# A third plain feature tile in each feed-forward, wide sums of its second half, and modulation weights in larger transfers

## The chip, the cores and the metric

The kernel runs on one core of a Trainium2 chip. The metric is the device time of one launch in microseconds (us), as the median of several runs. Besides, one execution was recorded by the hardware profiler; all rows below come from it. The engines are TensorE (PE: matmuls, with PEld for its weight loads), VectorE (DVE: elementwise operations), ScalarE (ACT: activations, copies, casts), GpSimd (POOL) and SyncE (SP: it issues the transfers, in order).

## What is computed

One step of a diffusion backbone of two layers, on 512 latent and 128 context tokens of width 1024, all in fp32. Each layer is a feed-forward (FFN), a mixer of three groups of heads, and a second FFN. Norm, shift, scale and gate of every part are modulated by vectors that come from a conditioning vector and a large matrix `w_ada`:

```python
def swiglu(x, w_in, w_out):
    g, u = jnp.split(x @ w_in, 2, axis=-1)
    return (jax.nn.silu(g) * u) @ w_out

def layer(h, mod, p, lam_init, ctx):
    sh1, sc1, gt1, sh2, sc2, gt2, sh3, sc3, gt3 = jnp.split(mod[:, None, :], 9, axis=-1)
    u = rmsnorm(h, p["g_norm"][0]) * (1.0 + sc1) + sh1
    h = h + 0.5 * gt1 * swiglu(u, p["w_ff_in"][0], p["w_ff_out"][0])
    ...
    y, cache = mix(u, p, lam_init, ctx)
    h = h + gt2 * y
    ...
    h = h + 0.5 * gt3 * swiglu(u, p["w_ff_in"][1], p["w_ff_out"][1])

for l in range(DEPTH):
    mod_ctx = jax.nn.silu(c_ctx)[None, :] @ w_ada[l] + b_ada[l]
    mod_lat = jax.nn.silu(c) @ w_ada[l] + b_ada[l]
```

Here x is 640 x 1024, w_in 1024 x 5632, w_out 2816 x 1024, and w_ada 1024 x 9216 per layer.

## The kernel before, in words

The four FFNs are called FFN0 to FFN3 here, in the order in which they run; FFN0 lies between the start and 537 us, FFN1 between 958 and 1436, FFN2 between 1436 and 1916, FFN3 between 2338 and 2806, and the two mixers between them.

Every matmul is done as three, on a high and a low part of both operands (`mm3`, L187): H x H, H x L, L x H. High parts are casts on ACT, low parts subtractions on DVE. So each operand, weight or activation, passes through ACT and DVE before PE can use it.

The first product of an FFN goes by 22 feature tiles f of 128 features (gate and up), in `GROUPS` of 6, 6, 5 and 5; after each group comes the second product of that group, in four steps of two output tiles (`unit2`). The 640 tokens are two halves of 320 (half 0, half 1), and the 1024 rows of the weights two halves of four k each. Two ways are used for a feature tile:

- *plain*, for tiles 0 and 1 of each FFN: eight quarter products, 96 matmuls of 320 columns. `plain0` does half 0 (from B11 and B21, 24 matmuls each, kk = 0 and 1), and `plain1` half 1 (from T1 and B22, 48 matmuls). `plain_copy` parks the result of B11 in the tiles `pm`, since half 1 needs it again; `plain_add` adds it. The weights are split in two pieces of 1024 columns (`split`).
- *wino*, for all others: seven products instead of eight, 84 matmuls, in exchange for sums of weights on DVE: seven splits of 512 columns (`split4`) and four sums of 512 columns (`weights`, L949).

What both need of the activations are sums too: `u_steps` (L761) makes them, for half 1 the tiles T1, B22, T3, T2, T4, each as a high and a low part, per k in pieces of 128 x 320. Plain tiles need T1 and B22 only, wino tiles all.

Before the first feature tile of FFN1, 2 and 3 the norm of half 1 isn't done yet. It is a generator, `self.pend`: its first step puts the sum of squares on PE (nst), its second puts the row of factors on PE (nbc) and then emits all `u_steps` (nx is the first operation on DVE). `ffn` takes the two steps between the chunks of `plain0`. After a plain product th is the tanh (ACT) and the gating (DVE, L685 and L686), hid the split of the result.

Modulation: 72 units of 256 columns of w_ada a layer are needed, 8 of them in the startup, others in two ways. A unit by P is eight *strips* on PE (`ada_strip`, adp<-adaw, one for each k, narrow weights of 32 columns), a copy by ACT (adrow) and two small matmuls that fold it (adt). A unit by D is 16 multiply-adds on DVE (adacc, L342 and L344), then transposes on PE (adt). Their weights come through `ada_raw` (L320) in the tiles adaw; the page counts 256 transfers of 256 KB. The table `ADA` gives, by FFN, at which feature tile (first entry) and at which step of the second product (second entry) `pump` emits units, and of which sort.

The order on each engine is set by a scheduler at build time (and in the startup by a planner of its own, with costs and due times); each engine runs its list in order. PE has two slots for the tiles gu, and the weights four slots each of H and L. SP issues transfers in order and waits where the buffer is still in use.

## Time and profile before

| | us |
|---|---|
| median of 3 runs (2825.23 to 2825.39) | 2825.35 |
| the profiled execution | 2820.54 |
| span of its trace | 2818.8 |
| PE busy | 2707.1 |
| DVE busy | 2158.1 |
| ACT busy | 1298.7 |
| POOL busy | 310.8 |

The span goes from the first to the last instruction; the profiled execution's own time is a little more. [...] In the timelines neighbouring instructions of a kind are one row with a count; a number in square brackets is the time that the engine stood idle before it, followed by what released it.

### The profile page before, as it was taken

How to read it: one execution, taken by the hardware profiler on the slowest of the kernel's cores; microseconds unless marked ns; L12 is line 12 of the kernel's file. 1: busy time of each engine (PE TensorE's matmuls, PEld its weight loads, DVE VectorE, ACT ScalarE, POOL GpSimd, SP SyncE). 2: the span in 40 equal slices, each digit the busy share in tenths (PEclk: the TensorE clock that was granted, in tenths of full speed). 3: DMA queues.
4: the chain of work that ended last, by engine and by line, in shares of the span. 5: the costliest groups of instructions: out<-in, count | busy, mean ns of one | idle time of the engine just before them, and what ended most of it. 6: DMA issues, size and time to landing. Idle time of an engine off the chain costs nothing.

```text
span 2818.8 us, 47166 instructions
## 1 busy us (share of the span) xinstructions
PE 2707.1 (96%) x17821; PEld 2526.0 (90%) x17821; DVE 2158.1 (77%) x4717; ACT 1298.7 (46%) x3001; POOL 310.8 (11%) x505
## 2 busy tenths in 40 slices
PE   6999999999989999999989999999999998999998
PEld 5799999888889889999979999997888897999998
DVE  6688889766865598899979989888667647776765
ACT  5324334456666352433444334345657634443433
POOL 1000000142522100000010000003343220000000
PEclk8999999999999999999999999999999999999999
DMA  8443443322102334343343433442211032322232
GB/s 241 143 143 113 128 124 112 113 92 87 39 3 81 93 94 131 91 120 117 109 120 105 120 117 99 133 129 83 82 49 38 3 109 79 90 75 75 83 83 76
DMA packets 365403, 276.47 MB, mean 98 GB/s; under 512 B 27176, under 2 KB 352888, under 8 KB 365176
## 3 DMA queue, kind: packets, MB, share of 16 engines
q1 hardware_dynamic: 365176, 273.46, 32.8%
q8 instruction: 141, 2.31, 0.4%
q14 instruction: 86, 0.70, 0.1%
HBM read 259.25 MB, written 14.16 MB: 97 GB/s over the span
## 4 chain that ended last, share of the span: by engine, by line
PE 80%; DVE 9%; DMA 4%; ACT 3%; issue 2%; POOL 2%; SPq 0%; DVEq 0%; POOLq 0%; ACTq 0%
PE gu L191 33%; PE w L191 17%; PE zps L191 6%; PE ga L191 5%; PE wo L191 4%; PE tr L1276 3%; PE y L191 3%; DMA adaw<-in_w_ada 3%; PE sc L191 2%; PE num L191 2%; DVE adacc L344 1%; PE adp L332 1%; PE z L191 1%; DVE h L928 1%; DMA out_new_b_n<-cst 1%
## 5 line engine op out<-in xcount | busy, mean ns | idle before, releaser
L191 PE MATMUL w<-hid,wH 128*128 128x384 f32 (+1 forms) x2816 | 625.2, 312 | 0.8 <-ACT hid L691 0.4
L191 PE MATMUL gu<-u,wH 128*128 128x320 f32 x3392 | 594.0, 316 | 28.2 <-DVE th L686 21.3
L191 PEld LDWEIGHTS gu<-u,wH 128*128 128x128 f32 x3392 | 519.8, 190 | 60.8 <-DVE th L686 22.5
L191 PE MATMUL gu<-u,wL 128*128 128x320 f32 x3136 | 548.5, 314 | 6.2 <-ACT X L1003 3.3
L191 PEld LDWEIGHTS gu<-u,wL 128*128 128x128 f32 x3136 | 479.9, 189 | 28.9 <-ACT X L1003 10.6
L191 PEld LDWEIGHTS w<-hid,wH 128*128 128x128 f32 x2816 | 472.5, 188 | 5.6 <-ACT hid L691 3.9
L191 PE MATMUL w<-hid,wL 128*128 128x256 f32 (+1 forms) x1408 | 433.5, 310 | 0.0
L344 DVE SCALAR_TENSOR_TENSOR adacc<-adaw,cs,adacc 128x256 f32<-128x256 f32 x602 | 269.5, 480 | 14.6 <-DMA adaw<-in_w_ada 11.0
L220 ACT CAST wH<-raw 128x512 fp32r<-128x512 f32 x280 | 172.4, 620 | 219.0 <-PE w L191 87.4
L191 PEld LDWEIGHTS w<-hid,wL 128*128 128x128 f32 x1408 | 265.0, 189 | 0.3
L220 ACT CAST wL<-raw 128x512 fp32r<-128x512 f32 x280 | 172.8, 620 | 167.7 <-PE gu L191 43.0
L736 POOL TENSOR_TENSOR ssum<-ssum,sq 128x384 f32<-128x384 f32 (+1 forms) x36 | 36.2, 1004 | 1914.4 <-ACT sq L735 1861.0
L191 PE MATMUL zps<-wH,u 128*128 128x512 f32 x704 | 244.2, 407 | 1.8 <-ACT u L885 1.7
L928 DVE SCALAR_TENSOR_TENSOR h<-w,mod,h 128x128 f32<-128x128 f32 (+1 forms) x384 | 154.9, 435 | 101.6 <-PE w L191 100.2
L221 DVE TENSOR_TENSOR wH<-raw,wH 128x512 fp32r<-128x512 f32 x280 | 191.8, 686 | 34.5 <-ACT wH L220 33.8
L221 DVE TENSOR_TENSOR wL<-raw,wL 128x512 fp32r<-128x512 f32 x280 | 191.9, 687 | 32.1 <-ACT wL L220 29.1
L211 ACT CAST wH<-raw 128x768 fp32r<-128x768 f32 (+2 forms) x140 | 112.2, 802 | 200.9 <-PE w L191 168.0
L191 PEld LDWEIGHTS zps<-wH,u 128*128 128x128 f32 x704 | 133.3, 190 | 33.8 <-ACT u L885 5.3
L691 ACT CAST hid<-th 128x320 fp32r<-128x320 f32 x176 | 80.9, 459 | 165.3 <-DVE th L686 165.3
L212 DVE TENSOR_TENSOR wL<-raw,wH 128x768 fp32r<-128x768 f32 (+2 forms) x140 | 127.7, 916 | 21.7 <-PE gu L191 15.9
L191 PE MATMUL zps<-wL,u 128*128 128x512 f32 x352 | 139.2, 395 | 0.0
L1684 DVE TENSOR_REDUCE mx<-sc 128x1 f32<-128x640 f32 (+1 forms) x160 | 110.7, 708 | 27.2 <-PE sc L191 26.8
(338 smaller groups left out, 4492.4 us busy)
## 6 DMA issues: line engine op xcount, KB each, us to landing
raw<-in_w_ff_in SPq DMA_DIRECT2D x176, 512.0 KB
adaw<-in_w_ada SPq DMA_DIRECT2D x256, 256.0 KB
raw<-in_w_ff_out SPq DMA_DIRECT2D x32, 768.0 KB
raw<-in_w_ff_out SPq DMA_DIRECT2D x32, 640.0 KB
rawi<-in_w_in SPq DMA_DIRECT2D x16, 1024.0 KB
adaw<-in_w_ada SPq DMA_DIRECT2D x16, 512.0 KB
rawo<-in_w_out SPq DMA_DIRECT2D x8, 1024.0 KB
bspill<-z SPq DMA_DIRECT2D x20, 256.0 KB
```

The lines of the kernel that those rows point to most:

```text
L191: self.nc.tensor.matmul(out, lhsT, rhs, start=start, stop=stop, skip_group_check=go_on)
L211: nc.scalar.copy(H, raw)
L212: nc.vector.tensor_tensor(L, raw, H.bitcast(F32), ALU.subtract)
L220: nc.scalar.copy(w[:, 0], raw)
L221: nc.vector.tensor_tensor(w[:, 1], raw, w[:, 0].bitcast(F32), ALU.subtract)
L332: self.nc.tensor.matmul(ps[j : j + 32, 0:256], self.cs32[:, k, :], raw, start=k < 4, stop=k >= 4, tile_position=(0, j))
L344: nc.vector.scalar_tensor_tensor(acc[v], raw, col, acc[v], ALU.mult, ALU.add)
L691: nc.scalar.copy(self.hid[q][:, 0, c], st["th", hf])
L736: (nc.gpsimd if d in SSG else nc.vector).tensor_tensor(ssum[:, :w], ssum[:, :w], sq[:, :w], ALU.add)
L928: nc.vector.scalar_tensor_tensor(hh, ps[:, s0:s1], gm[:, v, d : d + 1], hh, ALU.mult, ALU.add)
L1276: nc.tensor.transpose(pt[:, i * P : (i + 1) * P], x, ident)
L1684: nc.vector.tensor_reduce(bx["mx"], view(), AX.XY, ALU.max, negate=True)
```

## The change

It has five parts.

1. `NP_ = 3`: a third feature tile (f = 2) of each FFN is done plain. It comes behind the half 1 of tiles 0 and 1, and does its half 0 and half 1 in one go. The wino tiles start at f = 3. `plain_copy` takes its buffers by f % 2.
2. In `u_steps`, T3, T2 and their high and low parts, and those of T4, become one operation each over all four k (128 x 1280); t4 stays in four. All of them come behind all t1 and the low parts of B22. In the startup the tiles ua and ub become one tile each, since four k must lie side by side.
3. `ada_raw` takes four k in a transfer, 512 KB, two per unit, with two buffers instead of three. adacc and adrow have two buffers instead of three.
4. In `ffn` both steps of the half-1 norm are taken in the kk = 0 round, each behind a tile's `plain_copy`, so each is one chunk of 24 matmuls sooner.
5. The table `ADA`: four units together at tile 0 become one there and one each at tiles 2, 3 and 4 (FFN1 and FFN3); in FFN0 there is one at 0 and one at each tile from 2 to 10; in FFN2 they move to 4, 7 and 10. How many units go by P (21) and by D (43) stays.

```diff
@@ -33,11 +33,12 @@
 ADA = (
...
-    ({0: "PPPP", 8: "D", 14: "D", 19: "D"}, _OUT),
...
+    ({0: "P", **dict.fromkeys((2, 3, 4), "P"), 8: "D", 14: "D", 19: "D"}, _OUT),
...
+NP_ = 3
@@ -320,10 +321,10 @@
         c0 = s * D + u * 256
-        for e in range(0, KD, 2):
-            raw = self.adp.tile([P, 2, 256], F32, tag="adaw", name="adaw", bufs=3)
-            self.nc.sync.dma_start(raw, self.a["w_ada"][l, e * P : (e + 2) * P, c0 : c0 + 256].rearrange("(k p) c -> p k c", p=P))
-            for k in range(2):
+        for e in range(0, KD, QK):
+            raw = self.adp.tile([P, QK, 256], F32, tag="adaw", name="adaw", bufs=2)
+            self.nc.sync.dma_start(raw, self.a["w_ada"][l, e * P : (e + QK) * P, c0 : c0 + 256].rearrange("(k p) c -> p k c", p=P))
+            for k in range(QK):
                 yield e + k, raw[:, k, :]
@@ -569,7 +570,8 @@
-        xab = lambda n, k: xp.tile([P, UH], F32, name=f"{n}{k}")
+        xabt = {n: xp.tile([P, QK, UH], F32, name=n) for n in ("ua", "ub")}
+        xab = lambda n, k: xabt[n][:, k]
@@ -648,7 +650,7 @@
-        tags = (("m1", 1), ("X", 1)) if f == 0 else (("m7", 2), ("m7", 2))
+        tags = (("m1", 1), ("X", 1)) if f % 2 == 0 else (("m7", 2), ("m7", 2))
@@ -822,20 +824,20 @@
+        al = slice(0, QK)
+        every = lambda x: [(x, k) for k in range(QK)]
+        wa, wb = (lambda: ab("ua", al)), (lambda: ab("ub", al))
+        comb("t3", al, lambda: tt(wa(), wb(), wa(), ALU.subtract), *every("t1"), *every("LB22"))
+        hi("T3", al, wa, ("t3", al))
+        comb("t2", al, lambda: tt(wb(), wb(), b11, ALU.subtract), ("t3", al))
+        low("T3", al, wa, ("HT3", al))
+        hi("T2", al, wb, ("t2", al))
         for k in range(QK):
-            a, b = (lambda k=k: A[k]), (lambda k=k: B[k])
-            comb("t3", k, lambda a=a, b=b: tt(a(), b(), a(), ALU.subtract), ("t1", k), ("u", QK + k))
-            hi("T3", k, a, ("t3", k))
-            comb("t2", k, lambda b=b, k=k: tt(b(), b(), b11[:, k], ALU.subtract), ("t3", k), ("LB22", k))
-            low("T3", k, a, ("HT3", k))
-        for k in range(QK):
-            b, b2 = (lambda k=k: B[k]), (lambda k=k: b21[:, k])
-            comb("t4", k, lambda b=b, b2=b2, k=k: stt(b2(), b2(), bm(0, QK + k), b(), ALU.add, ALU.subtract), ("t2", k))
-            hi("T2", k, b, ("t2", k))
-            hi("T4", k, b2, ("t4", k))
-            low("T4", k, b2, ("HT4", k))
-        for k in range(QK):
-            low("T2", k, lambda k=k: B[k], ("HT2", k), *(("LT4", z) for z in range(QK)))
+            comb("t4", k, lambda k=k: stt(b21[:, k], b21[:, k], bm(0, QK + k), wb()[:, k], ALU.add, ALU.subtract), ("t2", al))
+        hi("T4", al, lambda: b21, *every("t4"))
+        low("T4", al, lambda: b21, ("HT4", al))
+        low("T2", al, wb, ("HT2", al), ("LT4", al))
@@ -1032,7 +1034,7 @@
-                fs = range(2, g1)
+                fs = range(NP_, g1)
@@ -1043,16 +1045,13 @@
                                 pl[f]["ps"] = self.ps2("gu")
-                            elif f == 1:
-                                next(self.pend)
                             for k in range(QK):
                                 self.plain0(pl[f], kk, k)
                             if kk == 0:
                                 self.plain_copy(pl[f], f)
+                                next(self.pend)
                             else:
                                 post(pl[f], 0)
-                        if kk == 0:
-                            next(self.pend)
@@ -1064,6 +1063,24 @@
+                for f in range(2, NP_):
+                    st = dict(q=f)
+                    raw = load1(f)
+                    st["W"] = [self.split(raw[:, s], [P, KD, P]) for s in range(2)]
+                    st["ps"] = self.ps2("gu")
+                    for kk in range(2):
+                        for k in range(QK):
+                            self.plain0(st, kk, k)
+                        if kk == 0:
+                            self.plain_copy(st, f)
+                    post(st, 0)
+                    ps = self.ps2("gu")
+                    st["ps1"] = [ps[:, s, :UH] for s in range(2)]
+                    for k in range(QK):
+                        self.plain1(st, k)
+                    self.plain_add(st)
+                    post(st, 1)
+                    self.pump(pin.get(f, ""))
```

Three places in the lists of the engines show what moves.

PE in FFN1, behind the last half-0 matmuls of tile 1; adp are strips, gu_11255 (before) and gu_11021 (after) the half 1 of tile 0, whose operands u_1102x to u_1103x and u_1086x are T1 and B22. Before:

```order
L191 MATMUL gu_10951<-u_10797,wH_10918 128x320
L191 MATMUL gu_10951<-u_10796,wL_10919 128x320
L332 MATMUL adp_11158<-adaw_11171,cs32_118 32x256 x2
L332 MATMUL adp_11183<-adaw_11184,cs32_118 32x256 x2
L332 MATMUL adp_11183<-adaw_11188,cs32_118 32x256 x2
L191 MATMUL gu_11255<-u_11030,wH_10903 128x320
L191 MATMUL gu_11255<-u_11031,wH_10903 128x320
L191 MATMUL gu_11255<-u_11030,wL_10904 128x320
L191 MATMUL adt_11177<-fold_120,adrow_11175 128x2 x2
L191 MATMUL gu_11255<-u_11028,wH_10903 128x320
L191 MATMUL gu_11255<-u_11029,wH_10903 128x320
L191 MATMUL gu_11255<-u_11028,wL_10904 128x320
```

And now:

```order
L192 MATMUL gu_10824<-u_10663,wH_10784 128x320
L192 MATMUL gu_10824<-u_10662,wL_10785 128x320
L333 MATMUL adp_11263<-adaw_11264,cs32_118 32x256 x4
L333 MATMUL adp_11263<-adaw_11270,cs32_118 32x256 x4
L192 MATMUL adt_11278<-fold_120,adrow_11276 128x2 x2
L333 MATMUL adp_11429<-adaw_11430,cs32_118 32x256 x4
L333 MATMUL adp_11429<-adaw_11436,cs32_118 32x256 x4
L192 MATMUL gu_11021<-u_10865,wH_10769 128x320
L192 MATMUL gu_11021<-u_10866,wH_10769 128x320
L192 MATMUL gu_11021<-u_10865,wL_10770 128x320
L192 MATMUL gu_11021<-u_10863,wH_10769 128x320
```

Before, strips came in pairs and the half-1 matmuls ran between them; now the strips of two units, with the fold of the first, stand ahead of the first half-1 matmul.

PE in FFN0, behind the startup; before, in the half 1 of tile 1 (gu_872), a unit of those at tile 0:

```order
L332 MATMUL adp_800<-adaw_801,cs32_118 32x256 x2
L191 MATMUL gu_872<-u_150,wL_557 128x320
L191 MATMUL gu_872<-u_148,wH_556 128x320
L332 MATMUL adp_800<-adaw_805,cs32_118 32x256 x2
L191 MATMUL gu_872<-u_149,wH_556 128x320
L191 MATMUL gu_872<-u_148,wL_557 128x320
L191 MATMUL gu_872<-u_150,wH_494 128x320
L191 MATMUL gu_872<-u_151,wH_494 128x320
L191 MATMUL gu_872<-u_150,wL_495 128x320
L191 MATMUL gu_872<-u_148,wH_494 128x320
L191 MATMUL gu_872<-u_149,wH_494 128x320
L191 MATMUL gu_872<-u_148,wL_495 128x320
```

Now, a unit pumped at a later tile, between two products of a wino tile:

```order
L333 MATMUL adp_1117<-adaw_1118,cs32_118 32x256 x4
L333 MATMUL adp_1117<-adaw_1124,cs32_118 32x256
L192 MATMUL gu_999<-u_157,wH_989 128x320
L192 MATMUL gu_999<-u_149,wH_989 128x320
L192 MATMUL gu_999<-u_157,wH_989 128x320 x2
L192 MATMUL gu_999<-u_149,wH_989 128x320
L192 MATMUL gu_999<-u_157,wH_989 128x320 x2
L192 MATMUL gu_999<-u_149,wH_989 128x320
L192 MATMUL gu_999<-u_157,wH_989 128x320 x2
L192 MATMUL gu_999<-u_149,wH_989 128x320
L192 MATMUL gu_999<-u_157,wH_989 128x320
L333 MATMUL adp_1117<-adaw_1124,cs32_118 32x256 x3
```

Pairs of strips with a few matmuls between them became a group of five (four and one), and one of three that follows twelve matmuls later.

ACT in FFN2, where half 1's sums are made; L791 before and L793 after are the casts of `u_steps` to high parts, L785 and L787 its scale and shift, wH casts of weights (tile 2). Before:

```order
L785 ACTIVATE hid_16187<-nx_16231,mod1_0_12166,mod1_1_12038 128x192
L791 CAST u_16180<-hid_15960 128x320
L791 CAST u_16178<-hid_16187 128x320
L791 CAST u_16183<-hid_16186 128x320
L358 COPY adrow_16372<-adp_16355 128x256
L220 CAST wH_16496<-raw_16493 128x512
L791 CAST u_16182<-hid_16187 128x320
L220 CAST wH_16503<-raw_16493 128x512
L791 CAST u_16183<-hid_16186 128x320 x2
L791 CAST u_16182<-hid_16187 128x320 x2
L791 CAST u_16183<-hid_16186 128x320
L791 CAST u_16185<-u_15961 128x320
```

And now:

```order
L787 ACTIVATE hid_15917<-nx_15958,mod1_0_11976,mod1_1_11852 128x192
L359 COPY adrow_16583<-adp_16570 128x256
L787 ACTIVATE hid_15918<-nx_15962,mod1_0_11976,mod1_1_11852 128x192
L793 CAST u_15911<-hid_15722 128x320
L793 CAST u_15909<-hid_15918 128x320
L212 CAST wH_16163<-raw_16160 128x1024
L212 CAST wH_16167<-raw_16160 128x1024
L793 CAST u_15914<-hid_15917 128x1280
L793 CAST u_15913<-hid_15918 128x1280
L693 CAST hid_16043<-th_16039 128x320
L683 ACTIVATE th_16097<-pm_15859 128x320
L793 CAST u_15916<-u_15723 128x1280
```

The eight casts of T3 and T2 became two of 1280 columns, and the two casts of 1024 columns for the weights of the third plain tile stand ahead of them.

## Rows read from the trace of the kernel before

**Rows 1.** The page: span; busy us, share and instructions of PE and DVE.

```profile
span 2818.8 us, 47166 instructions
PE 2707.1 (96%) x17821; PEld 2526.0 (90%) x17821; DVE 2158.1 (77%) x4717; ACT 1298.7 (46%) x3001; POOL 310.8 (11%) x505
```

**Rows 2.** Waits of PE: who waited, for whom, total us, times, longest.

```profile
PE gu L191 <- DVE th L686: 21.3, 3, 7.8
...
PE adt L191 <- ACT adarow L558: 10.7, 7, 3.4
```

**Rows 3.** Timeline of PE: start, us, operation, count, idle before, releaser.

```profile
1002.81 0.64 PE L191 MATMUL gu<-u,wH 128*128 128x320 f32 x1 [6.75 <-DVE th L686]
...
1479.38 0.63 PE L191 MATMUL gu<-u,wH 128*128 128x320 f32 x1 [7.80 <-DVE th L686]
...
2382.92 0.64 PE L191 MATMUL gu<-u,wH 128*128 128x320 f32 x1 [6.76 <-DVE th L686]
```

**Rows 4.** Windows: length; busy by engine; granted clock; DMA share; GB/s.

```profile
978.70:984.00 5.30, 4.34 (x31) 2.94 (x27) 4.33 (x12) 2.31 (x6) 0.00 (x0) 1.00 0.60 173
1000.00:1008.00 8.00, 5.19 (x21) 5.19 (x22) 7.08 (x23) 1.39 (x3) 0.00 (x0) 0.50 0.00 0
1008.00:1010.00 2.00, 2.00 (x13) 2.00 (x12) 2.00 (x6) 0.00 (x0) 0.00 (x0) 0.81 0.03 8
```

**Rows 5.** Windows of FFN0, same columns.

```profile
76.45:108.00 31.55, 31.10 (x206) 21.48 (x206) 16.94 (x39) 10.54 (x23) 0.00 (x0) 1.00 0.64 183
160.00:205.00 45.00, 45.00 (x310) 45.00 (x309) 43.92 (x105) 7.95 (x12) 0.00 (x0) 1.00 0.52 147
```

**Rows 6.** Timeline of PE in FFN1.

```profile
983.64 0.62 PE L332 MATMUL adp<-adaw,cs 128*32 128x256 f32 x4 [0.96 <-DMA adaw<-in_w_ada]
...
1010.05 0.46 PE L191 MATMUL gu<-u,wH 128*128 128x320 f32 x2
...
1013.57 2.31 PE L191 MATMUL gu<-u,wH 128*128 128x320 f32 x12
```

**Rows 7.** Timeline of DVE in FFN1.

```profile
974.82 0.48 DVE L777 TENSOR_TENSOR nx<-h,nbc 128x320 f32<-128x320 f32 x1
...
999.07 1.29 DVE L797 TENSOR_TENSOR u<-u 128x320 fp32r<-128x320 f32 x3
```

**Rows 8.** Forms of DVE, 958 to 1030 us: count, busy us, mean ns.

```profile
L797 DVE TENSOR_TENSOR u<-hid,u 128x320 fp32r<-128x320 f32 x16 | 7.2, 485 | 5.8 <-ACT u L791 5.8
...
L212 DVE TENSOR_TENSOR wL<-raw,wH 128x1024 fp32r<-128x1024 f32 x3 | 3.7, 1217 | 0.0
...
L783 DVE TENSOR_SCALAR hid<-nx,mod,mod 128x128 f32<-128x128 f32 x8 | 2.7, 340 | 0.0
...
L820 DVE SCALAR_TENSOR_TENSOR hid<-hid,mod 128x320 f32<-128x320 f32 x4 | 2.2, 544 | 0.0
```

**Rows 9.** Forms of PE, 76.45 to 108 us, strips and fold.

```profile
L332 PE MATMUL adp<-adaw,cs 128*32 128x256 f32 x76 | 10.9, 390 | 0.4 <-DMA adaw<-in_w_ada 0.4
...
L191 PE MATMUL adt<-fold,adrow 128*128 128x2 f32 x16 | 2.0, 230 | 0.0
```

**Rows 10.** Timeline of PE in FFN1, groups of strips.

```profile
978.04 1.06 PE L332 MATMUL adp<-adaw,cs 128*32 128x256 f32 x12
...
988.08 0.62 PE L332 MATMUL adp<-adaw,cs 128*32 128x256 f32 x2
```

**Rows 11.** Timeline of PE in the startup.

```profile
53.20 1.02 PE L191 MATMUL adt<-fold,adarow 128*128 128x2 f32 x4 [3.40 <-ACT adarow L558]
```

**Rows 12.** Timeline of ACT, then SP, in FFN1.

```profile
984.32 0.37 ACT L358 COPY adrow<-adp 128x256 f32<-128x256 f32 x1 [3.20 <-PE adp L332]
...
990.88 0.37 ACT L358 COPY adrow<-adp 128x256 f32<-128x256 f32 x1 [2.14 <-PE adp L332]
...
978.70 17.77 SPq L325 DMA_DIRECT2D adaw<-in_w_ada  x13
```

**Rows 13.** Waits of DVE at line 344, the units it runs itself.

```profile
DVE adacc L344 <- DMA adaw<-in_w_ada: 11.0, 17, 1.8
```

More of the change, by code (lines that the diff above doesn't have):

```diff
@@ L35 @@
 ADA = (
-    ({0: "PPPP", **dict.fromkeys((2, 3, 4, 5, 9, 15), "P"), 8: "D", 14: "D", 19: "D"}, _OUT),
-    ({0: "PPPP", 8: "D", 14: "D", 19: "D"}, _OUT),
-    ({0: "PPP", 4: "D", 8: "D", 14: "D", 19: "D"}, _OUT),
-    ({0: "PPPP"}, {}),
+    ({0: "P", **dict.fromkeys(range(2, 11), "P"), 14: "D", 16: "D", 19: "D"}, _OUT),
+    ({0: "P", **dict.fromkeys((2, 3, 4), "P"), 8: "D", 14: "D", 19: "D"}, _OUT),
+    ({**dict.fromkeys((4, 7, 10), "P"), 8: "D", 13: "D", 16: "D", 19: "D"}, _OUT),
+    ({0: "P", **dict.fromkeys((2, 3, 4), "P")}, {}),
 )
+NP_ = 3
 GROUPS = ((0, 6), (6, 12), (12, 17), (17, 22))
@@ L336, in ada_unit @@
         pt = self.ps1("adt")
-        acc = [self.adp.tile([P, 256], F32, tag="adacc", name="adacc", bufs=3) for v in range(2)]
+        acc = [self.adp.tile([P, 256], F32, tag="adacc", name="adacc", bufs=2) for v in range(2)]
         for k, raw in self.ada_raw(l, s, u):
@@ L356, in ada_unit_pe @@
             self.ada_strip(ps, k, raw)
-        row = self.adp.tile([P, 256], F32, tag="adacc", name="adrow", bufs=3)
+        row = self.adp.tile([P, 256], F32, tag="adacc", name="adrow", bufs=2)
         self.nc.scalar.copy(row, ps[:, 0:256])
@@ L790, in hi @@
         def hi(n, k, src, *deps):
-            add(("H" + n, k), "A", UH, lambda e: nc.scalar.copy(uc[n][0][:, k], src()), *deps)
+            add(("H" + n, k), "A", UH if k != slice(0, QK) else QK * UH, lambda e: nc.scalar.copy(uc[n][0][:, k], src()), *deps)
         def low(n, k, src, *deps):
@@ L797, in f @@
                 nc.vector.tensor_tensor(uc[n][1][:, k], src(), uc[n][0][:, k].bitcast(F32), ALU.subtract)
-            add(("L" + n, k), "D", UH, f, *deps)
+            add(("L" + n, k), "D", UH if k != slice(0, QK) else QK * UH, f, *deps)
         def comb(n, k, fn, *deps):
-            add((n, k), "D", UH, lambda e: fn(), *deps)
+            add((n, k), "D", UH if k != slice(0, QK) else QK * UH, lambda e: fn(), *deps)
         if hf == 0:
```

## The prediction

> **What bounds the kernel now.** The page comes first: TensorE (PE) is busy 96% of the span, VectorE (DVE) 77% [rows 1]. So only two things pay: less work on PE, or fewer of the places where PE stands still. Next the waits of PE, to see how few those places are: three stops of `gu` behind DVE `th` add up to 21.3 us, adt behind ACT in the startup 10.7 [rows 2]. The timeline then shows where the three stops lie: one at the start of each of FFN1, FFN2 and FFN3, 6.75, 7.80 and 6.76 us, each time ahead of the half-1 product of feature tile 1 [rows 3]. [...] Last come two stretches away from the starts: 76.45 to 108 us (98% PE) and 160 to 205 us, where PE is busy throughout but DVE 43.92 of 45 us [rows 5]. The second will matter for a rival.
>
> **Unit prices.** A matmul of 320 columns: 24 of them stand between the rows at 1010.05 and 1013.57, 3.52/24 = 0.147 us [rows 6]. DVE operations back to back start closer than their busy time: three of 320 columns take 1.29 us and one is busy 485 ns, so the next starts after 0.405 [rows 7, 8]. By the same 0.08 off, L783 (340 ns) counts 0.26 and L820 (544 ns) 0.46; 1024 columns are busy 1217 ns [rows 8]: a slope of 1.04 ns a column, so 1280 columns are busy an estimated 1.48 us and start 1.40 apart.
>
> **A modulation unit by strips (P).** In 76.45 to 108 us PE ran 206 instructions: 76 adp, 16 adt, the other 114 matmuls of 320 columns [rows 5, 9]. 114 x 0.147 = 16.8; 31.55 - 16.8 - 0.4 (wait for the transfer, in the adp row) = 14.4 us for 76/16 = 4.75 units (the trace counts two PE instructions a strip): 3.0 us a unit. The surprise is what sets this price: two strips (x4) take 0.62 us, even one (x2) 0.62, six (x12) only 1.06 [rows 6, 10]. Every switch from matmuls to strips and back costs about half a microsecond. The order shows units before in four groups of two or, at later tiles, groups of 5, 1 and 2 strips; after, 8 in one group, or 5 and 3. At 0.11 us a further strip, 8 cost 1.28, 5 and 3 cost 0.95 + 0.73 = 1.68, four pairs 2.48, and 5, 1, 2 cost 2.19. What is over in the 3.0 (0.55) is adt and its switches, unchanged.
>
> **FFN0.** PE doesn't stop after the startup, so here only its work counts. The four units at tile 0 go to 5 and 3: 4 x 0.8 = 3.2. Six others from 5, 1, 2 to 5 and 3: 6 x 0.5, and 6 x 0.1 for a switch less, 3.6. Against it the third plain tile: 96 matmuls instead of 84, 12 x 0.147 = 1.8 us. Gain **5.0** (4.5 to 6.5). On DVE a plain tile takes two splits of 1024 (2.4 us) for seven of 512 and four sums, by the slope 0.69 each or 7.5, some 5 us less [rows 8]; PE doesn't wait for DVE here, so I book nothing.
>
> **Startup.** PE stands 3.40 us at 53.20 behind ACT's adarow and 10.7 us over seven such waits [rows 2, 11]. The order puts the last adt there earlier, in front of merged DVE work. The nearest bounds are nothing and the whole 3.40 plus about a microsecond of matmuls that come sooner; I take **3** (0 to 4.6), since the matmuls behind it already have their operands.
>
> **FFN1 and FFN3.** Three edits meet here. (a) The norm of half 1 is advanced one chunk of 24 matmuls, 3.5 us: nx, 974.82 before [rows 7], now about 971.3. (b) Before, strips were strewn through half 1, and ACT, in order, stood 3.20 and 2.14 us at adrow copies for strips not yet run [rows 12]; its casts behind them kept DVE waiting. Now T1 and B22 come first without them: per k two nx, two L783, one L820 and two low parts, 0.81 + 0.52 + 0.46 + 0.81 = 2.6 us, x4 = 10.3, so **ready at 981.6** against about 997. (c) But the order now has, ahead of the first half-1 matmul, 8 strips, adt, and 8 more strips. The second 8 need 1 MB in two transfers, which SP can only issue when the first 8 have freed both buffers, about 979. Before, 13 issues began at 978.70, and PE waited for the second pair until 983.64: 4.9 us for 512 KB [rows 6, 12]; at the 173 GB/s of this stretch [rows 4] 1 MB takes 6.1 us, the last issue stands near 980, so the strips end near 986.9. The stop thus doesn't vanish: about 5 us of it return as waiting for a transfer.
> [...]
> From 986.9: 2 x 48 half-1 matmuls, then the third plain tile with 96: 192 x 0.147 = 28.2; half a clock again, 2.5 (0 to 3.1); the fourth unit, pumped later, 2.2: **1019.8**. Before, the 48 matmuls from 1002.81 end at 1013.57 [rows 6], half a microsecond's wait for the weights and 84 x 0.147 = 12.3 lead to 1026.4. Gain **6.6** (0 to 14). FFN3 has the same stop, order and numbers: **6.6**.
>
> **FFN2.** Units now stand at tiles 4, 7, 10 instead of three at 0, so no strips lie in the start, but DVE becomes the bound: T1 and B22 done about 1462, both plain half-1 products done by 1472. What holds PE is what stands on DVE ahead of their pm additions: T3, T2, their low parts, t4, T4. On ACT the two 1024-column casts of tile 2 stand ahead of the T3 cast, and wait for weight buffers of tile 0. Adding up the order from there, PE stands still about 6 us in pieces between 1472 and 1479.5, and tile 2 ends at 1494.2 with 1.9 for the clock; 5.3 of units and switches come later: 1499.5 against 1501.3 before (1479.38 + 48 x 0.147 + 0.6 adt + 2 clock + 12.3). Gain **2** (-2 to 5).
> Merging four operations of 320 columns into one saves 4 x 0.405 - 1.40 = 0.2 us by the rows, 1 us an FFN for five.
> [...]
>
> **Sum:** 5.0 + 3 + 6.6 + 2 + 6.6 = 23.2 us. The profiled execution took 2820.54 (span 2818.8), which gives 2797; its distance to the median of the three runs, 2825.35, is carried along: **2802**.
>
> **Rivals.** (1) *The starts re-form.* If each stop only changes its name (1 MB of transfer, adt behind adrow, DVE in FFN2, then the lower clock), FFN1 to 3 give nothing; 5 + 3 remain: 2817. For it: PE's stop in FFN1 is only delayed by 5 us in my own sum. Against it: 15 us sooner T1 and B22 is much to eat up.
> (2) *The transfers land in time.* If strips run before T1 and B22 are ready, 5 us less in each of FFN1 and FFN3, and without a stop no lower clock, 2.5 each: 15 more, 2787. Against it: rows 6 show PE waiting on just this with smaller transfers.
> (3) *Slower: units by DVE (D) starve on bigger transfers.* 43 units go this way, 33 of them in the second products, where DVE has 45 - 43.92 = 1.08 us to spare in 45 with three units [rows 5]: 0.36 a unit. A half unit of four k is 8 DVE operations of 0.40, 3.2 us; 512 KB took 4.9. If a half's transfer starts only when the other half begins, DVE waits 1.7 a half-unit, 1.4 over the slack, and PE waits through adt and the updates: 33 x 1.0 = 33 us against my 23: 2835. It decides from 0.36 us a unit. Already before, DVE waited 11.0 us, 17 times, at L344 [rows 13]. Against it: 1 MB is now in flight instead of 768 KB, and PE waited but little for it.
>
> **Chances.** Forecast 0.58 (2795 to 2810), (1) 0.22 (2811 to 2824), (2) 0.12 (2783 to 2794), (3) 0.08 (2824 to 2840). A measurement tells 0.2%, 5.6 us, from no change: faster is below 2819.7. Of (1), a third lies within that: same 0.08, slower 0.07, faster 0.85. The range takes in most of (1) and (2): 2786 to 2823.
>
> **What would show it.** After: the strips' groups in FFN0 fewer and the stretch 76 to 108 cheaper; nx in FFN1 3 to 4 us sooner relative to the FFN's first matmul; a PE wait at adp on adaw of some 5 us in FFN1 and FFN3 in place of gu behind th; in FFN2 small gu waits behind pm; L344 waits no longer than 15 us in all. If no wait on adaw shows, (2) holds; if L344 waits treble and PE waits at adt, (3); if a half clock lasts longer than 6 us at each start, (1).

## The result

The changed kernel takes 2793.63 us (median, 2793.09 to 2795.42); the kernel before, beside it, 2825.29. The ratio is 0.9892 (95% interval 0.9874 to 0.9909), 31.7 us less. Measured once more, beside the last experiments (below), it is 0.988 (0.9863 to 0.9897). The profiled execution took 2793.09 against 2820.54, 27.45 us less.

The page of after (span; busy time of the engines):

```profile
span 2791.3 us, 46818 instructions
PE 2700.6 (97%) x17869; PEld 2533.9 (91%) x17869; DVE 2128.1 (76%) x4618; ACT 1285.6 (46%) x2941; POOL 308.6 (11%) x504
```

PE is busy 6.5 us less [rows 1], with 48 matmuls more, and idle 21 us less (span less busy time, 111.7 before and 90.7 after). The waits of PE after:

```profile
PE adp L333 <- DMA adaw<-in_w_ada: 9.0, 8, 2.7
PE adt L192 <- ACT adarow L559: 8.6, 7, 2.2
...
PE adt L192 <- ACT adrow L359: 3.7, 4, 1.4
PE gu L192 <- DVE pm L669: 3.7, 1, 3.7
```

The 21.3 us of `gu` behind `th` [rows 2] are gone; 3.7 behind `pm` (FFN2) and 3.7 behind adrow are new. Lengths of the four FFNs in the traces, from the first `gu` matmul (FFN0 to the first matmul of the mixer, with most of the startup's second half in it), in us:

| kernel | ratio to before (95%) | FFN0 | FFN1 | FFN2 | FFN3 |
|---|---|---|---|---|---|
| before | 1 | 499.0 | 478.0 | 479.4 | 480.8 |
| after | 0.9892 (0.9874, 0.9909) | 491.6 | 470.5 | 473.4 | 471.2 |
| after again, e11 | 0.9880 (0.9863, 0.9897) | 491.9 | 468.4 | 473.9 | 474.0 |
| e1: two plain tiles | 0.9872 (0.9857, 0.9887) | 487.8 | 468.8 | 475.9 | 473.5 |
| e2: 256 KB, 3 buffers | 0.9962 (0.9949, 0.9975) | 499.8 | 477.8 | 476.8 | 477.5 |
| e3: old table | 0.9869 (0.9847, 0.9892) | 487.3 | 468.1 | 471.8 | 471.9 |
| e4: old place of the norm | 0.9911 (0.9894, 0.9927) | 490.9 | 473.2 | 474.9 | 476.8 |
| e5: before + 512 KB | 0.9916 (0.9901, 0.9930) | 492.3 | 472.6 | 474.9 | 476.6 |
| e6: nothing merged | 0.9963 (0.9950, 0.9976) | 496.6 | 475.6 | 475.5 | 480.1 |
| e7: units at 3, 4, 5 | 0.9896 (0.9881, 0.9911) | 490.9 | 469.9 | 473.5 | 472.9 |
| e8: mix | 0.9860 (0.9842, 0.9877) | 485.5 | 466.2 | 475.1 | 472.7 |
| e9: pieces, merged order | 0.9940 (0.9923, 0.9957) | 492.4 | 475.7 | 476.9 | 480.6 |
| e10: 256 KB, 4 buffers | 0.9883 (0.9868, 0.9898) | 493.9 | 467.9 | 473.7 | 476.2 |
| e12: mix, units in bunches | 0.9850 (0.9835, 0.9864) | 485.6 | 466.0 | 474.5 | 472.6 |

Two traces of one kernel, after and e11, tell how far a single length can be trusted: FFN0 and FFN2 agree within 0.5 us, FFN1 and FFN3 swap 2 to 3 us. What differs stands in the windows. Each FFN1 and FFN3 starts with a stop of 1.80 us before its strips (as before). In the 6 us from 2 us after the start, FFN1 and then FFN3, of after and then of e11 (third from the end TensorE's granted clock, as a share of full speed):

```profile
953.70:959.70 6.00, 4.51 (x32) 3.94 (x33) 5.38 (x11) 1.14 (x4) 1.58 (x1) 0.77 0.47 134
2322.14:2328.14 6.00, 4.51 (x41) 3.94 (x41) 5.38 (x11) 1.14 (x4) 1.58 (x1) 1.00 0.47 137
```

```profile
955.64:961.64 6.00, 4.51 (x41) 3.94 (x41) 5.38 (x11) 1.13 (x4) 1.58 (x1) 1.00 0.44 134
2321.68:2327.68 6.00, 4.51 (x32) 3.94 (x33) 5.38 (x11) 1.14 (x4) 1.58 (x1) 0.77 0.45 133
```

After the same stop the granted clock was 0.77 over these 6 us in one FFN (0.50 from 957.70 to 959.70) and 1.00 in the other, and the other way round in the second trace: 9 instructions fewer in 6 us. The mixers, which the change doesn't touch, differ too: both together take 843.6 us in the trace of before, 846.8 in after and 847.0 in e11, so of the 30.4 us that the four FFNs gain in the traces some 3 don't show in the whole. At least in part it is the clock again: after a stop of 2.41 us the ten transposes took 1.56 us before, at a granted clock of 1.00, and 2.40 after, at 0.50.

```profile
896.97 1.56 PE L2158 MATMUL yt<-ident,qa 128*128 128x128 f32 x10 [2.41 <-DVE u L2168]
```

```profile
889.29 2.40 PE L2175 MATMUL yt<-ident,qa 128*128 128x128 f32 x10 [2.41 <-DVE u L2185]
```

So differences of 2 to 3 us in FFN1 or FFN3 are not read below.

### The profile page after: what moved, and what is told of

Read it like the earlier page. It is cut to its first block, busy times and chain, and to the rows that moved or that the text cites. A ratio compares the mean times of both kernels' runs of the same rounds, so it can differ in the third digit from the quotient of the medians.

```text
span 2791.3 us, 46818 instructions
## 1 busy us (share of the span) xinstructions
PE 2700.6 (97%) x17869; PEld 2533.9 (91%) x17869; DVE 2128.1 (76%) x4618; ACT 1285.6 (46%) x2941; POOL 308.6 (11%) x504
## 4 chain that ended last, share of the span: by engine, by line
PE 86%; DVE 6%; ACT 3%; DMA 2%; POOL 2%; issue 1%; SPq 0%; POOLq 0%; DVEq 0%; ACTq 0%
PE gu L192 35%; PE w L192 20%; PE zps L192 6%; PE ga L192 5%; PE wo L192 4%; PE tr L1293 3%; PE y L192 3%; PE sc L192 2%; PE num L192 2%; PE z L192 1%; PE adp L333 1%; DMA out_new_b_n<-cst 1%; PE adt L348 1%; DMA adaw<-in_w_ada 1%; PE st L192 1%
## 5 line engine op out<-in xcount | busy, mean ns | idle before, releaser
L192 PE MATMUL gu<-u,wH 128*128 128x320 f32 x3504 | 624.8, 316 | 8.3 <-DVE pm L669 3.7
L192 PEld LDWEIGHTS gu<-u,wH 128*128 128x128 f32 x3504 | 541.9, 190 | 33.9 <-ACT X L1005 7.9
L192 PE MATMUL gu<-u,wL 128*128 128x320 f32 x3120 | 565.6, 314 | 2.4 <-DVE wL L213 1.1
L192 PEld LDWEIGHTS w<-hid,wH 128*128 128x128 f32 x2816 | 471.8, 188 | 7.3 <-ACT hid L693 3.4
L221 ACT CAST wH<-raw 128x512 fp32r<-128x512 f32 x266 | 163.6, 620 | 205.5 <-PE w L192 91.8
L345 DVE SCALAR_TENSOR_TENSOR adacc<-adaw,cs,adacc 128x256 f32<-128x256 f32 x602 | 255.0, 477 | 0.0
L221 ACT CAST wL<-raw 128x512 fp32r<-128x512 f32 x266 | 163.9, 620 | 167.1 <-PE gu L192 55.7
L212 ACT CAST wH<-raw 128x640 fp32r<-128x640 f32 (+2 forms) x148 | 120.4, 816 | 226.1 <-PE w L192 165.6
L222 DVE TENSOR_TENSOR wH<-raw,wH 128x512 fp32r<-128x512 f32 x266 | 182.0, 686 | 41.5 <-ACT wH L221 39.8
L222 DVE TENSOR_TENSOR wL<-raw,wL 128x512 fp32r<-128x512 f32 x266 | 182.0, 686 | 38.4 <-ACT wL L221 37.3
L213 DVE TENSOR_TENSOR wL<-raw,wH 128x640 fp32r<-128x640 f32 (+2 forms) x148 | 137.4, 931 | 28.8 <-PE gu L192 14.7
```

The lines of the kernel that those rows point to most:

```text
L192: self.nc.tensor.matmul(out, lhsT, rhs, start=start, stop=stop, skip_group_check=go_on)
L212: nc.scalar.copy(H, raw)
L213: nc.vector.tensor_tensor(L, raw, H.bitcast(F32), ALU.subtract)
L221: nc.scalar.copy(w[:, 0], raw)
L222: nc.vector.tensor_tensor(w[:, 1], raw, w[:, 0].bitcast(F32), ALU.subtract)
L345: nc.vector.scalar_tensor_tensor(acc[v], raw, col, acc[v], ALU.mult, ALU.add)
```

## The experiments

**e1, the third plain tile.** `NP_ = 3` set back to 2.

```diff
-NP_ = 3
+NP_ = 2
```

> The changed kernel with two plain tiles again, all else kept. Theory A (the third plain tile is 12 matmuls of 0.147 us more in each of the four FFNs, and pays only where VectorE is late): where nothing waits for VectorE, each FFN gets 1.8 us shorter, so FFN0 1.8 less; in FFN1, FFN2 and FFN3 tile 2 again needs seven weight splits and T2 to T4 directly behind the half-1 products of tiles 0 and 1, and TensorE waits 2 to 5 us there: in all 2795 to 2805. Rival B (the tile is a pure cost, VectorE would have been done anyway): 4 x 1.8 = 7 us less, 2787.

Measured 2791.32, ratio 0.9872; the interval overlaps those of after, so the tile as a whole is worth nothing that can be told. The lengths say why: FFN0 3.8 us shorter without it, FFN1 within what the clock moves, FFN2 2.5 longer, FFN3 2.3 or less. It costs where PE is the bound and pays about as much where DVE is late. Theory A has the signs right, but its range (2795 to 2805) is missed; that the tile pays in sum is not shown.

**e2, the transfers.** 256 KB again, with three buffers of adaw, adacc and adrow.

```diff
-        for e in range(0, KD, QK):
-            raw = self.adp.tile([P, QK, 256], F32, tag="adaw", name="adaw", bufs=2)
+        for e in range(0, KD, 2):
+            raw = self.adp.tile([P, 2, 256], F32, tag="adaw", name="adaw", bufs=3)
...
```

> The changed kernel with transfers of 256 KB, three buffers of them, and three of adacc and adrow again. Theory A (the price of a unit by strips is the number of switches; the larger transfer makes groups of 5 and 3 of what was 5, 1, 2 or pairs): 21 units lose 0.5 to 0.8 us each, 10 to 16 us; VectorE's waits for adaw return (15 us in all before) but hide: 2800 to 2810. Rival B (what matters is that less lies in flight: 768 KB instead of 1 MB, and at the start of FFN1 and FFN3 a smaller first transfer lands sooner): the starts gain up to 2 us each, units by VectorE lose a little: 2790 to 2796.

Measured 2815.79, ratio 0.9962: some 20 us slower than after, more than theory A's upper end, and far from B. It is work, not waiting: PE is busy 20.7 us more than in after, and no wait of `gu` behind `th` comes back.

```profile
PE 2721.3 (97%) x17869; PEld 2542.2 (90%) x17869; DVE 2134.2 (76%) x4618; ACT 1285.3 (46%) x2941; POOL 308.6 (11%) x504
```

In FFN0, where PE hardly waits, it is 8.1 us for 30 groups of strips behind the startup instead of 19: 0.74 us a group. In the whole kernel there are 57 groups instead of 37, by that price 15 us; the rest, most of it in FFN1 and FFN2, is not accounted for. A unit of a later tile in e2, and one of after:

```profile
2407.99 1.05 PE L333 MATMUL adp<-adaw,cs 128*32 128x256 f32 x10
...
2410.92 0.62 PE L333 MATMUL adp<-adaw,cs 128*32 128x256 f32 x2
...
2412.26 0.63 PE L333 MATMUL adp<-adaw,cs 128*32 128x256 f32 x4
```

```profile
104.12 1.05 PE L333 MATMUL adp<-adaw,cs 128*32 128x256 f32 x10
...
107.07 0.63 PE L333 MATMUL adp<-adaw,cs 128*32 128x256 f32 x6
```

DVE's waits for adaw returned too (line 345 is line 344 of before), but not longer than there [rows 13]:

```profile
DVE adacc L345 <- DMA adaw<-in_w_ada: 8.6, 13, 1.3
```

**e10, the same transfers, four buffers.** This parts the size of a transfer from what is in flight. (adacc and adrow keep their two buffers, as in after; e2 had given them three again, so e2 and e10 differ in that too.)

```diff
-            raw = self.adp.tile([P, QK, 256], F32, tag="adaw", name="adaw", bufs=2)
+            raw = self.adp.tile([P, 2, 256], F32, tag="adaw", name="adaw", bufs=4)
...
```

> The changed kernel with transfers of 256 KB but four buffers of them, so that 1 MB, a whole unit, is in flight as in the changed kernel; its strips stand in 40 groups behind the startup, against 37 there and 57 with three buffers. Theory A (what pays is that a whole unit's weights are in the buffers, which lets the strips stand in few groups; each group costs TensorE about 0.8 us): 3 x 0.8 = 2.4 us slower than the changed kernel, 2794 to 2799, ratio 0.989 to 0.991. Rival B (what pays is the size of a transfer): as with three buffers, 2812 to 2818, ratio 0.996.

Measured 2797.05, ratio 0.9883, beside after again at 0.988 on the same chip. With 256 KB a transfer all that e2 lost is back. So it isn't the larger transfer that pays but the fourth buffer: a whole unit, 1 MB, fits, the scheduler can put its strips together (40 groups, against 57 in e2 and 37 in after), and PE changes over less often.

**e5, the transfers alone.** The kernel before with the edit of `ada_raw`, and two buffers of adacc and adrow, as in the change.

> The kernel before with one part of the change alone: transfers of 512 KB, two buffers each of adaw, adacc and adrow. Theory A (each separate group of strips costs TensorE about 0.8 us beside the strips themselves, and the larger transfer brings the groups behind the startup from 66 to 37): 29 x 0.8 = 23 us less than before, ratio 0.992. Rival B (the parts need each other: without the new table and the sooner norm the starts of FFN1 to FFN3 stay bound by VectorE, and only FFN0 gains): 8 us less, 0.997.

Measured 2802.18, ratio 0.9916, theory A's value. This one part, of which the prediction spoke as a cheaper unit, brings three quarters of the whole gain. PE is busy 17.2 us less than before [rows 1]; the groups behind the startup are 37 instead of 66. The starts are not healed by it: the 21.3 us of `gu` behind `th` [rows 2] are 16.1 here, at FFN1 and FFN3, and FFN2's stop has another name, 5.0 behind `mod`.

```profile
PE 2689.9 (96%) x17821; PEld 2524.8 (90%) x17821; DVE 2147.9 (77%) x4717; ACT 1299.5 (46%) x3001; POOL 309.7 (11%) x505
```

```profile
PE gu L191 <- DVE th L686: 16.1, 2, 8.0
...
PE adt L191 <- DVE mod L371: 5.0, 1, 5.0
```

**e3, the table.** The four lines of `ADA` of the kernel before; that of FFN1:

```diff
...
-    ({0: "P", **dict.fromkeys((2, 3, 4), "P"), 8: "D", 14: "D", 19: "D"}, _OUT),
+    ({0: "PPPP", 8: "D", 14: "D", 19: "D"}, _OUT),
...
```

> The changed kernel with the old table of units, so four (three in FFN2) together at tile 0. Theory A (strips at the start of an FFN stand between TensorE and its half-1 products, and their adrow copies hold ScalarE's casts up): FFN1, FFN2 and FFN3 each lose 3 to 7 us, FFN0 1 to 3 by smaller groups: 2802 to 2815. Rival B (the units fill holes in which TensorE would wait for T1 and B22 anyway, so it doesn't matter where they stand): within 2 us of 2794.

Measured 2789.81, ratio 0.9869 (0.9847 to 0.9892): theory A is refuted, the old table is not slower; rival B is nearer, though its reason, holes at the starts, doesn't explain what FFN0 does. FFN0 is even 4.3 us shorter with the old table. There four units by P fewer stand in group 2 of its tiles (80.7 instead of 90.2 us from the first to the last `gu` matmul, 2.4 a unit) and three more in group 1 (109.4 instead of 104.1, 1.8 a unit): together they are done in groups of four and eight strips, spread ones in five and three.

**e4, the norm.** The two `next(self.pend)` at their old places.

> The changed kernel with the half-1 norm taken at its old places, one chunk of 24 matmuls (3.5 us) later. Theory A (T1 and B22 gate the restart of TensorE in FFN1 to FFN3): nx comes 2.5 to 3.5 us later; in FFN1 and FFN3 about 3 us of that are covered by the strips that wait for their transfer until 979.5 us while T1 and B22 are ready at 976.6, so FFN1 and FFN3 lose 0 to 1 us each, FFN2, which is bound by VectorE, 2.5 to 3.5: 2796 to 2799. Rival B (each microsecond shows): 3 x 3 = 9 us, 2803.

Measured 2801.66, ratio 0.9911; between the two theories. The lengths say 2.7, 1.5 and 5.6 us in FFN1 to FFN3 (about 2 of uncertainty in the first and last). PE waits for `pm` on DVE 10.8 us in three places there, 3.7 in one in after:

```profile
PE gu L192 <- DVE pm L669: 10.8, 3, 3.7
```

But the order of the strips moved with the norm: behind the startup they stand in 47 groups there, not 37, ten in each of FFN1 and FFN3 instead of five. At 0.74 us a group that is 3.7 in each of the two, so how much of the loss there is the norm's and how much the groups' isn't told apart. In FFN2, where the groups are as many as in after, the norm one chunk later costs 1 to 1.5 us.

**e7, one unit later.** In FFN1 and FFN3 the units of tiles 2, 3, 4 at 3, 4, 5; the line of FFN1:

```diff
-    ({0: "P", **dict.fromkeys((2, 3, 4), "P"), 8: "D", 14: "D", 19: "D"}, _OUT),
+    ({0: "P", **dict.fromkeys((3, 4, 5), "P"), 8: "D", 14: "D", 19: "D"}, _OUT),
...
```

> The changed kernel with the units of FFN1 and FFN3 at tiles 0, 3, 4 and 5 instead of 0, 2, 3 and 4. TensorE then has 8 strips and one adt ahead of the first half-1 product, not 16 strips. Theory A (the second 8 strips wait 2.2 and 1.5 us for their transfer and themselves take 2, and the stop brings the lower clock): TensorE restarts 3 to 4 us sooner in FFN1 and FFN3, less lower clock on top, the unit costs 2.4 later: 2 to 6 us less in all, 2788 to 2792. Rival B (T1 and B22 or VectorE hold the restart anyway): no change, 2794.

Measured 2796.92, ratio 0.9896: no change, as rival B had it. The second 8 strips and their wait are gone from FFN1's start, and another wait has taken most of their place, `gu` behind `th` (timeline of PE in e7). PE does restart sooner, 25.2 us after the first `gu` of FFN1 and of FFN3, where after has 27.8 and 26.1; the unit that comes later costs as much or more, 2.4 us by theory A's own price.

```profile
973.16 1.07 PE L333 MATMUL adp<-adaw,cs 128*32 128x256 f32 x16 [0.93 <-PE gu L192]
...
978.01 0.90 PE L192 MATMUL gu<-u,wH 128*128 128x320 f32 x2 [2.68 <-DVE th L688]
```

**e6, the merging.** The loops over k of the kernel before for T3, T2 and T4, all else as after.

> The changed kernel with T3, T2, T4 and their parts per k again, 128 x 320. Theory A (merging saves VectorE 0.2 us for each of five operations, by start to start): FFN2, which is bound by VectorE, 1 us slower, FFN1 and FFN3 0 to 1, 2794 to 2797. [...] Rival C (merged operations wait for all four k and stand in the way of th and pm, so pieces are better): 2 to 6 us faster.

Measured 2816.07, ratio 0.9963: 20 us slower, where theory A gave 2794 to 2797 and rival C a gain. Here it is waiting, not work: PE is busy 1.9 us more than in after and idle 22 more. The waits name it:

```profile
PE 2702.5 (96%) x17869; PEld 2535.0 (90%) x17869; DVE 2133.0 (76%) x4677; ACT 1290.4 (46%) x2977; POOL 310.4 (11%) x505
```

```profile
PE gu L192 <- DVE th L688: 19.3, 3, 7.3
```

Three stops behind `th` are back, with sooner norm, new table, large transfers and third tile all in place; in FFN1 and FFN3 they now lie ahead of the half 1 of tile 0, where before has them ahead of that of tile 1. And e6 is 14 us slower than e5 (2802.18, beside it on the same chip), which has the large transfers and none of the other parts: without the merging, the norm, the table and the third tile together do harm. And in the startup FFN0's first group is 4.2 us longer, which is what the prediction had put down to the startup.

**e9, pieces in the merged order.** Is it the order of the T operations or their length? All t3 behind all t1 and the low parts of B22, then all casts, and so on, but each in four pieces:

```diff
-        comb("t3", al, lambda: tt(wa(), wb(), wa(), ALU.subtract), *every("t1"), *every("LB22"))
-        hi("T3", al, wa, ("t3", al))
+        for k in range(QK):
+            comb("t3", k, lambda k=k: tt(A[k], B[k], A[k], ALU.subtract), *every("t1"), *every("LB22"))
+        for k in range(QK):
+            hi("T3", k, A1(k), *every("t3"))
...
```

> The changed kernel with T3, T2, T4 and their parts in pieces of 128 x 320 again, but in the order of the merged ones: all t3 behind all t1 and the low parts of B22, then all casts, then all t2, and so on. Undoing the merging with the old order cost 20 us. Theory A (what paid was the order: T1 and B22 and the gating of tile 1 no longer stand behind the T3 chain on VectorE, and the start of the weights does not): 1 us per FFN for 0.2 us more an operation, 2796 to 2800, ratio to before 0.990 to 0.9915. Rival B (the length of the operations paid): as with the old order, 2812 to 2818, ratio 0.996.

Measured 2812.45, ratio 0.994: close to rival B, and theory A has fallen. The startup's 4 us stay (FFN0 492.4), so there the order was enough; FFN1 to FFN3 are as slow as with nothing merged. Four operations of 0.405 instead of one of 1.40, five times, are 1.1 us an FFN; that doesn't make the 5 to 7 in FFN1 and 6 to 9 in FFN3 (against either trace of after). The timelines of DVE show what does. FFN3 of e9:

```profile
2352.71 0.48 DVE L834 TENSOR_TENSOR hid<-hid 128x320 f32<-128x320 f32 x1
...
2353.92 1.28 DVE L834 TENSOR_TENSOR hid<-hid 128x320 f32<-128x320 f32 x3
2355.12 1.69 DVE L838 TENSOR_TENSOR hid<-hid 128x320 f32<-128x320 f32 x4
2356.73 1.69 DVE L799 TENSOR_TENSOR u<-hid,u 128x320 fp32r<-128x320 f32 x4
...
2362.20 1.68 DVE L799 TENSOR_TENSOR u<-hid,u 128x320 fp32r<-128x320 f32 x4
2363.80 0.47 DVE L688 TENSOR_TENSOR th<-th,gu 128x320 f32<-128x320 f32 x1
```

FFN3 of after:

```profile
2343.44 1.48 DVE L831 TENSOR_TENSOR hid<-hid 128x1280 f32<-128x1280 f32 x1
2344.84 0.48 DVE L688 TENSOR_TENSOR th<-th,gu 128x320 f32<-128x320 f32 x1
2345.24 1.48 DVE L833 TENSOR_TENSOR hid<-hid 128x1280 f32<-128x1280 f32 x1
```

and what PE does about it in e9:

```profile
2364.33 0.90 PE L192 MATMUL gu<-u,wH 128*128 128x320 f32 x2 [5.93 <-DVE th L688]
```

L688 (L686 of before) is the last reader of the first tile's `gu`, and PE has two slots of them. In after it stands behind one T operation, 1.4 us after the start of T3; in e9 behind all of them, 11 us after (2352.71 to 2363.80). So what the merging pays with is a place in the list. Why the scheduler chose so is only argued: a merged t3 must be done, and cast by ACT as a whole, before its low part can run, and `th` goes into that hole; four pieces follow each other without a hole, and `th` is put last. That its place is the cause of the stops rests on these rows; a kernel with pieces and `th` put in front by hand was not tried.

**e8 and e12, a mix.** Old table, two plain tiles in FFN0 and FFN1 and three in FFN2 and FFN3 (e8); the same, with FFN0's six single units in two bunches of three (e12):

```diff
+NP_ = (2, 2, 3, 3)
...
-                fs = range(NP_, g1)
+                fs = range(NP_[2 * l + j], g1)
...
```

```diff
-    ({0: "PPPP", **dict.fromkeys((2, 3, 4, 5, 9, 15), "P"), 8: "D", 14: "D", 19: "D"}, _OUT),
+    ({0: "PPPP", 2: "PPP", 4: "PPP", 8: "D", 14: "D", 19: "D"}, _OUT),
```

> The changed kernel with the old table of units (four at tile 0 together), and three plain tiles in FFN2 and FFN3 only, two in FFN0 and FFN1. Theory A (the spread table costs 4, 2.5 and 1.5 us in FFN0, FFN1 and FFN2 by what its undoing gave there; the third plain tile costs 3.8 and 1.7 us in FFN0 and FFN1 and brings 2 to 2.5 each in FFN2 and FFN3): 8 to 13 us under the changed kernel, ratio to before 0.985. Rival B (both undoings gain from the same waits, so the gains don't add): as the better of the two, 5 to 7 us under, 0.987.

> The mix with two plain tiles in FFN0 and FFN1, three in FFN2 and FFN3, and the old table, but with the six single units of FFN0 (tiles 2, 3, 4, 5, 9, 15) in bunches of three at tiles 2 and 4. Their strips then stand in groups of four, not five and three. Theory A (a group's price goes in steps: up to four strips 0.64 us, up to eight 1.07, by the traces so far): five units save 0.4 us each, 2 us less than the mix, 2782 to 2786, ratio 0.9855. Rival B (3 MB at once are late and TensorE waits for them, or the tiles' own weights come late): 2 to 10 us more than the mix, 0.987 to 0.990.

> The changed kernel once more, on the chip and beside the runs of the others here, so that differences of 5 us can be read: ratio to before 0.989 as at first, by every theory.

e8: 2786.02, ratio 0.986 (theory A's values are 0.985 and 8 to 13 us; in the traces 7.6). e12: 2787.84, ratio 0.985 (0.9835 to 0.9864), beside after again at 2797.14 and 0.988 (0.9863 to 0.9897) on the same chip: 9.3 us less; the intervals just touch, and each run of e12 is faster than every run of after beside it. So the mix with bunches beats both kernels. The bunches as such bring nothing that shows, neither theory's value: FFN0 is 485.6 against 485.5, though its groups of four are cheap:

```profile
103.95 0.64 PE L333 MATMUL adp<-adaw,cs 128*32 128x256 f32 x8
106.33 0.64 PE L333 MATMUL adp<-adaw,cs 128*32 128x256 f32 x8 [0.38 <-DMA adaw<-in_w_ada]
```

By the prices of groups (below) those of e12 save 1.8 us in FFN0; what takes that back was not found.

## Why the prediction was right, and where by chance

The forecast was 23 us, the runs say 31.7, the two profiled executions 27.5. The direction and the outer range hold. The median lies just below the forecast's own band (2795 to 2810) and inside that of rival (2), whose mechanism did not come. That the sum is near is in part luck: FFN1 to FFN3 gave 23.1 us where 15.2 were forecast, the parts within FFN0 came out otherwise and cancelled, and the mixers, at nothing in the forecast, took some 3 back.

- **What bounds the kernel.** Right in kind, less work between groups on PE and fewer stops at the three starts, but wrong in shares. I put 15.2 of 23.2 us on the starts. The transfers alone (e5) give 25 us by fewer groups, with all three starts still stopped: 6.7 in FFN0 and 5.4, 4.5 and 4.1 in FFN1 to FFN3, where groups had no term of their own. From e5 to the whole change it is 8.6 us by the medians.
- **Unit prices.** The matmul, the DVE operations and 1280 columns (estimate 1.48 us and 1.40 between starts; row 1.48, next start 1.41 later) were right. For strips the straight line of 0.11 us a strip was wrong: the price goes in steps (below), so 5 and 3 cost 1.05 + 0.63, and 4 and 4 only 0.64 twice.
- **FFN0 and startup.** 8 forecast, 7.7 measured, but 4.1 of it in the startup (the first strips behind it at 72.29 against 76.38) and 3.6 in FFN0. Undone one at a time, the transfers are worth 8.1 there (e2), and the spread table costs 4.3 (e3) and the third tile 3.8 (e1), where I had booked 1.8 for the tile and, with the transfers, a gain of 3.2 for the four units that the table moves. The startup's rows show the adt sooner, as forecast:

```profile
50.93 1.01 PE L192 MATMUL adt<-fold,adarow 128*128 128x2 f32 x4 [1.42 <-ACT adarow L559]
```

- **FFN1 and FFN3.** 6.6 each forecast, 7.5 and 9.6 measured (9.6 and 6.8 in the second trace). The steps, relative to FFN1's first `gu`: nx at 14.0 instead of 16.5, 2.6 sooner (3.5 forecast); T1 and B22 done at 24.9 (23.3 forecast); PE through the strips at 27.8 (28.6 forecast), with 2.2 us of waiting for the transfer (1.5 in FFN3) where about 5 were forecast; and a granted clock of 0.50 from 978 to 984, 0.96 in the 4 us behind it:

```profile
965.68 0.89 DVE L779 TENSOR_TENSOR nx<-h,nbc 128x320 f32<-128x320 f32 x2 [2.46 <-PE nbc L192]
...
975.73 0.88 DVE L799 TENSOR_TENSOR u<-hid,u 128x320 fp32r<-128x320 f32 x2
...
977.94 0.48 DVE L688 TENSOR_TENSOR th<-th,gu 128x320 f32<-128x320 f32 x1
```

```profile
972.62 1.07 PE L333 MATMUL adp<-adaw,cs 128*32 128x256 f32 x16
975.07 0.61 PE L192 MATMUL adt<-fold,adrow 128*128 128x2 f32 x4 [1.37 <-ACT adrow L359]
976.92 0.64 PE L333 MATMUL adp<-adaw,cs 128*32 128x256 f32 x8 [1.24 <-DMA adaw<-in_w_ada]
978.46 1.08 PE L333 MATMUL adp<-adaw,cs 128*32 128x256 f32 x8 [0.91 <-DMA adaw<-in_w_ada]
```

```profile
978.00:984.00 6.00, 5.54 (x25) 4.73 (x26) 6.00 (x12) 3.99 (x5) 0.00 (x0) 0.50 0.55 175
984.00:988.00 4.00, 4.00 (x28) 4.00 (x27) 3.69 (x4) 0.87 (x3) 0.00 (x0) 0.96 0.00 0
```

  The forecast's terms for the clock, 2.5 us in each of these two FFNs and 1.9 in FFN2, no run shows as they stand. In their place, at a granted 0.50, after has 17 matmuls in the 4.70 us from the restart at 979.47 in FFN1, 12 in 3.37 from 2346.19 in FFN3 and 20 in 5.57 from 1463.30 in FFN2; against 0.147 us a matmul that is, as an estimate, 2.2, 1.6 and 2.6 us lost.

  The step that failed is a reason. I said that PE restarts when T1, B22 and the strips are ready, and gave the merging 1 us an FFN. But PE also needs a free `gu` slot, which `th` gives back, and it is the merging that puts `th` early enough: without it (e6, e9) FFN1 loses 5 to 7 and FFN3 6 to 9 us, in spite of the norm and the strips. The row that said so was there: the stops of before name `th`, not T1 or B22 [rows 3]. I had read `th` as late because it stood behind the T chain, and not asked what would put it in front. The time that I gave T1 and B22 before, about 997, was a misreading too: the part that ends there is one of T3. The last low parts of T1 and B22 ended at 988.99 (30.7 after the first `gu`, so the change gained 5.8 and not the 15 of which the rivals speak), and PE had used them for all of tile 0's half 1 by 994.80. The tanh of tile 1 was done at 978.58, and DVE came to its last gating at 1002.28. ACT, DVE twice, then PE of before:

```profile
978.14 0.44 ACT L681 ACTIVATE th<-gu 128x320 f32<-128x320 f32 x1 [0.17 <-PE gu L191]
```

```profile
988.10 0.89 DVE L797 TENSOR_TENSOR u<-hid,u 128x320 fp32r<-128x320 f32 x2
...
1002.28 0.48 DVE L686 TENSOR_TENSOR th<-th,gu 128x320 f32<-128x320 f32 x1
```

```profile
994.80 1.26 PE L332 MATMUL adp<-adaw,cs 128*32 128x256 f32 x8
```

- **FFN2.** 2 forecast, 6.0 measured (5.5 in the second trace). The transfers alone give 4.5 of it (e5), which had no term. The stop was sized 6 us; it is 3.69 and 0.34, the longer one behind `pm` as forecast:

```profile
1458.90 0.42 PE L192 MATMUL gu<-u,wL 128*128 128x320 f32 x1 [0.34 <-DVE wL L213]
...
1463.30 0.90 PE L192 MATMUL gu<-u,wH 128*128 128x320 f32 x2 [3.69 <-DVE pm L669]
```

- **The rivals.** That the starts re-form (2817) didn't happen; with the merging undone it does (e6, e9). e2 comes to nearly the same time without it: there PE restarts 27.2 us after the first `gu` of FFN1, as in after. That transfers land in time: no, and e7 shows that PE would then have waited for `th`. That units by DVE starve on larger transfers: the opposite, DVE's waits at this line went from 11.0 us [rows 13] to none:

```profile
L345 DVE SCALAR_TENSOR_TENSOR adacc<-adaw,cs,adacc 128x256 f32<-128x256 f32 x602 | 255.0, 477 | 0.0
```

Of the five parts, one carries most of the gain: a whole unit in flight, 25 us alone (e5) and some 20 when undone (e2), as less busy time of PE. The other four together bring 8.6 more. Among them the merging is worth some 20 us when undone, as less waiting, but most of that only makes good what the norm, the table and the third tile cost without it (e6 against e5). The norm when undone costs 8, in part by groups of strips, and the third tile and the table cost about what they bring or more. So the undone amounts don't add up to the whole; what the merging alone does to the kernel before was not tried.

## What to carry to other kernels

Read what a wait names before what the change is about: the stop named `th`, and undoing the part that moved `th` in the list cost 20 us where its saving in instruction time is 4.4 (1.1 an FFN). Where a scheduler lays the order, one longer operation in place of four can move what other engines wait for, so look at the order and not only at the operations' lengths. Small matmuls that interrupt a stream cost here by the number of interruptions (0.74 us a group in FFN0 of e2), so give them buffers enough to run in one piece. And an amount by undoing is not an amount by adding: build the part alone too.
